# Eight columns fewer in the expert lists, and a looped general path, in a two-layer PEER decoder

## Chip, cores and metric

The kernel runs as one program on one core of one Trainium2 chip. Its time is the device time of one execution in microseconds (us). TensorE (PE) does matrix products from a stationary and a moving operand and adds them up in accumulators of 128 x 512 fp32; VectorE (DVE), ScalarE (ACT) and GpSimd (POOL) do the rest; DMA queues fed by SyncE (SP), ACT and POOL move data between DRAM and the core. Every engine runs its own list of instructions in order and waits on semaphores.

## The reference

Two post-norm layers on 256 tokens of width 1024, all in fp32. Layer 0 mixes tokens with a state-space block, layer 1 with attention; the change touches neither. Each mixer is followed by a PEER block: 16384 experts, each a row `u` and a row `v` of 1024 numbers. Every token picks 16 experts for each of 8 heads by product keys, and adds up their `v` rows, weighted with the gate and with gelu(x . u):

```python
best, pos = lax.top_k(cand, PEER_TOPK)
expert = jnp.take_along_axis(cidx, pos, axis=-1)
gate = jax.nn.softmax(best, axis=-1)
u_g = u[expert]
v_g = v[expert]
act = jax.nn.gelu(jnp.einsum('td,thkd->thk', xb, u_g).astype(f32))
return jnp.einsum('thk,thkd->td', (gate * act).astype(v_g.dtype), v_g)
```

A layer norm and a gated input (`x + sigmoid(x @ w_gate) * (p @ w_proj)`) end the layer.

## The kernel before

The program is mixer, `peer(0)`, mixer, `peer(1)`. In `peer` the 16384 experts are 128 columns of 128. A matrix of fp32 is always split into a high and a low half, `hi` by a cast on ScalarE and `lo` by a subtraction on VectorE (`split`, L124 and L125), and a product is three matmuls, high by high, high by low, low by high (`mm3`, L149).

**The u phase.** `expert_in(e)` (L908) runs for all 128 columns: it loads 512 KB of `u` over SP's queue, splits it, multiplies it with the tokens into one of four accumulators (`halves`, L161, 16 matmuls), and ScalarE copies the two halves of the accumulator out (L916, L917), POOL adds them with a DMA (L918), and gelu follows. Routing and gating run beside it. Matmuls at L979 mark which experts of the first `MANY` columns any token uses, with `MANY` as their width.

**The lists.** `listing` (L1018) puts the used experts of the first `MANY` columns into lists of three classes: used by both blocks of 128 tokens, by the first alone, by the second alone. A list is cut into groups of 128 experts; `CAPS` says how many groups a class has (38, 23 and 23), `BASES` where each class starts. The steps of `listing` are spread by hand over the last columns of `expert_in` and the first dense columns (`stages`, L1235).

**The v phase.** All output is accumulated in four accumulators, two blocks of tokens by two halves of the width. A column at or above `MANY` is dense: `dense(e)` (L1243) loads all its 128 rows of `v` (512 KB over SP's queue, `expert_load`), splits them and its weights, and multiplies, 12 matmuls of 128 x 512 (`expert_out`). A group is gathered: POOL issues two indirect DMAs, for the weight rows and for the 128 rows of `v` (`fetched`, L1175), both are split, and a group of class both takes 12 matmuls, one of the other classes 6 (`group_out`). There are four buffers for loaded rows, four for split ones and six for gathered rows.

**The order of the v phase** is a list of steps sorted by a fraction from 0 to 1 (`emit`, `spread_over`). The first `LEAD` (6) dense columns follow the u phase; then the groups of class one with `MIX` (13) dense columns among them; then the groups of class both and class two with the remaining dense columns, and among those, at set fractions, the loads of the layer norm's input and of seven matrices of the gate projection (`gate_load`), a branch hint at 0.04 and the branch at 0.1. The last five groups of class two come after that (`TAIL`), with the layer norm of the first block of tokens ahead of their matmuls.

**The branch** (L1210) reads a flag: if the lists were too short for the experts used, `general()` adds the surplus from all `MANY` columns. With this input the lists suffice, and the branch goes around it on every engine. Its body is a Python loop, so its 96 turns of 12 matmuls stand one after another in TensorE's list of instructions. `hint` marks for TensorE, ScalarE and VectorE where the branch will be and that it is likely taken.

```python
def branch(_):
    with self.after(self.pace.marks):
        surplus = nc.values_load(picked["flag"][:1, :1], min_val=0, max_val=1)
    with self.tc.If(surplus > 0, preferred_fallthrough_block=True, label=f"over{i}"):
        general()
    self.pace.marks = ()
```

Of the kernel before, what the change touches and what calls it, by code (L numbers as in the profile page):

```python
# [8 lines left out]
F32R = mybir.dt.float32r  # L9
F16 = mybir.dt.float16  # L10
U32 = mybir.dt.uint32
AF = mybir.ActivationFunctionType
# [5 lines left out]
P = 128  # L18
T = 256
# [6 lines left out]
TAIL = 5  # L26
TURNS = (3, 4, 1, 2)
SPLIT = ((0, 0), (0, 1), (1, 0))
MANY = 96
ROUTED = 56  # L30
GATED = 116
DIRECT = ROUTED - 8
LEAD = 6
MIX = 13
CAPS = (38, 23, 23)
BASES = (0, 38, 61)
GROUPS = sum(CAPS)
TOP = 32768.0

# [27 lines left out]
class Net:  # L67
# [73 lines left out]
    def plain(self, src):  # L141
        raw = self.raw()
        dma = self.nc.sync.dma_start(raw, src)
        self.pace.marks = (dma.ins,)
        return raw

    def mm3(self, out, lhs, rhs, start, stop):
        for i, (a, b) in enumerate(SPLIT):
# [236 lines left out]
    def tl(self, shape, tag, bufs, dt=F32):  # L385
        return self.pool.tile(shape, dt, tag=tag, bufs=bufs, name=self.name(tag))
# [364 lines left out]
    def peer(self, i):  # L751
        nc, dram = self.nc, self.dram
        with self.tc.tile_pool(name=f"peer{i}", bufs=1) as pool, ExitStack() as stack:
# [262 lines left out]
            picked = {}  # L1016
# [135 lines left out]
            def expert_load(e, w=None):  # L1152
                return weights(e) if w is None else w, self.chunk(dram["v"][i, e])

            def expert_out(w, hl, start):
                for tb in range(2):
                    for h in range(2):
                        self.mm3(accs[tb][h], lambda a: w[:, a, tb * P:(tb + 1) * P],
                                 lambda b: hl[:, b, h * 512:(h + 1) * 512], start, False)

            def fetched(s, hl=None):
                n = picked["n"] = picked["n"] + 1
# [24 lines left out]
                return kind, w, hl  # L1187

            def group_out(kind, w, hl, ends=()):
                for n, tb in enumerate(((0, 1), (0,), (1,))[kind]):  # L1190
                    for h in range(2):
                        self.mm3(accs[tb][h], lambda a: w[:, a, n * P:n * P + P],
                                 lambda b: hl[:, b, h * 512:(h + 1) * 512], False, tb in ends)

            def group(s):
                group_out(*group_load(s), (0,) if s == closing else ())

            def general():
                for c in range(MANY):
                    raw, part, some = x[:, c % 2], pp[:, c % 2, :T], pp[:, c % 2, T:2 * T]  # L1200
                    hl = wide[0][:, c % 2]
                    w = wide[0][:, 2 + c % 2, 0].rearrange("p (a t) -> p a t", a=4)[:, :2]
                    nc.scalar.dma_start(part, table[1 + c * P:1 + c * P + P, :])
                    nc.scalar.dma_start(raw, dram["v"][i, c])
                    nc.scalar.activation(some, part, AF.Identity, scale=picked["over"][:, c:c + 1])
# [11 lines left out]
            for hc in range(19):  # L1217
# [6 lines left out]
                if hc >= 7:  # L1224
# [10 lines left out]
            stages = [[classes], [*sums, ranks], [], [places, ones[0]], ones[1:3], ones[3:5], ones[5:7], ones[7:9], ones[9:11],  # L1235
                      [ones[11], surplus], [keys, one], [], [two], [both]]
# [6 lines left out]
            def dense(e):  # L1243
                if not begun:
                    begun.append(e)
                    accs.extend(self.accs())
                expert_out(*expert_load(e, ready.pop(e, None)), e == MANY)

            main = [lambda e=e: expert_in(e) for e in range(GATED, P)] + [lambda e=e: dense(e) for e in range(MANY, MANY + LEAD)]
            for n, step in enumerate(main):  # L1250
                step()
                if n == P - GATED - 1:
                    with self.after(self.pace.marks):
                        ready[MANY] = weights(MANY)
                with self.after(self.pace.marks):
                    for f in stages[n] if n < len(stages) else []:
                        f()
                    if n >= P - GATED + 3 and lates:
                        lates.pop(0)()
                    if n >= 2 and n % 3 and todo:  # L1260
                        todo.pop(0)()
# [32 lines left out]
            wide = [new([P, 4, 2, 1024], "wide", F32R)]  # L1294
            pgw = {}

            def gate_load(n):
                if len(wide) <= n // 4:
                    wide.append(tl([P, 4, 2, 1024], F32R, "high"))
                raw = (x, pp)[n // 2][:, n % 2] if n < 4 else None  # L1300
                pgw[divmod(n, 4)] = self.chunk(dram["w_pg"][i, n], hl=wide[n // 4][:, n % 4], raw=raw)

            loads = [(0.65, lambda: nc.sync.dma_start(x, self.x_d[i])), (0.7, lambda: nc.sync.dma_start(pp, self.pp_d[i])),
                     (0.75, lambda: self.load_gb(gb0, 2 * i + 1))]
            loads += [(at, lambda n=n: gate_load(n)) for n, at in enumerate((0.25, 0.35, 0.45, 0.55, 0.88, 0.92, 0.96))]
            emit(inner, spread_over(dense, range(MANY + LEAD + MIX, P), 0.86), [(at, extra, f) for at, f in loads],
                 [(0.04, hint, None), (0.1, branch, None)])
            end = []
            for k, s in enumerate(last):
                end.append(group_load(s, None if k else wide[1][:, 3]))  # L1310
# [141 lines left out]
```

## Time and profile before

| | us |
|---|---|
| median of 3 runs | 1874.46 (1873.03 to 1877.22) |
| profiled execution | 1863.86 |
| span of its profile | 1862.1 |
| TensorE busy in it | 1814.2 (97%) |
| VectorE, ScalarE, POOL busy | 1492.6, 1152.3, 629.7 |

The v phase of layer 0 runs from 667 to about 950 us of the span, that of layer 1 from 1553 to about 1836. In rows of groups and timelines, L149 with `acc<-hl,w` is a matmul of the v phase; `raw`, `hl` and `w` are the loaded rows, the split rows and the split weights. What stands in brackets is how long the engine was idle ahead of that row and what ended the wait: an engine with a name, a DMA, "issue" for idle time in which it waited for nothing that the profile shows, and PEq for TensorE's own sequencer. A window's "(x112)" counts the instructions in it, and PEclk is the share of full clock granted to TensorE.

### The profile page before, as it was taken

The page shows a single profiled execution, that of the slowest core. Times are in us where ns is not written, and L with a number is a line of the kernel's source. Part 1 is how long each engine was busy: PE and PEld are TensorE (multiplying, and loading weights), DVE is VectorE, ACT ScalarE, POOL GpSimd, SP SyncE. Part 2 cuts the span into 40 slices and gives each one's busy share as a digit, 9 for nine tenths or more (in the row PEclk, how much of TensorE's full clock was granted, in tenths as well). Part 3 has the DMA queues.
Part 4 walks back from the last instruction along what each step waited for, and adds up shares of the span by engine and source line. Part 5 has one row for each costly group of instructions (what it writes and reads, how often), then busy time and mean ns, then how long its engine had stood idle before and what let it go on. Part 6 is the DMA issues. An engine that isn't in the chain of part 4 may idle for free. (4 is left out here: it accounts for less than half of the span.)

```text
span 1862.1 us, 31749 instructions
## 1 busy us (share of the span) xinstructions
PE 1814.2 (97%) x11112; PEld 1542.1 (83%) x11112; DVE 1492.6 (80%) x2936; ACT 1152.3 (62%) x2330; POOL 629.7 (34%) x620
## 2 busy tenths in 40 slices
PE   8999999999999999799989999999999999989997
PEld 7998888888888877588878788888888887768876
DVE  7798789989989987466766878998998998747665
ACT  6865456696666656455646655669666666646553
POOL 0001013232222247767700001333222225767671
PEclk9999999999999999899999999999999999989999
DMA  7555669897699998888825556989779999889871
GB/s 271 201 184 186 215 184 228 216 249 192 185 281 332 287 303 282 274 299 301 271 104 193 198 189 185 228 217 248 198 184 278 332 283 316 284 269 316 293 228 61
DMA packets 217904, 444.29 MB, mean 239 GB/s; under 512 B 18980, under 2 KB 126664, under 8 KB 216072
## 3 DMA queue, kind: packets, MB, share of 16 engines
q1 hardware_dynamic: 75208, 266.75, 42.6%
q0 software_dynamic: 67648, 137.66, 28.7%
q10 hardware_dynamic: 74880, 37.75, 7.0%
q8 instruction: 91, 1.49, 0.3%
q14 instruction: 77, 0.63, 0.1%
HBM read 364.46 MB, written 44.08 MB: 219 GB/s over the span
## 5 line engine op out<-in xcount | busy, mean ns | idle before, releaser
L125 DVE TENSOR_TENSOR hl<-raw,hl 128x1024 fp32r<-128x1024 f32 x570 | 695.0, 1222 | 226.5 <-ACT hl L124 161.2
L161 PE MATMUL acc<-xT,hl 128*128 128x256 f32 (+1 forms) x4608 | 840.7, 340 | 1.4 <-DVE xT L188 0.8
L161 PEld LDWEIGHTS acc<-xT,hl 128*128 128x128 f32 x4608 | 700.6, 188 | 101.2 <-DVE hl L125 4.3
L124 ACT CAST hl<-raw 128x1024 fp32r<-128x1024 f32 x570 | 597.9, 1052 | 247.3 <-PE acc L149 105.9
L149 PE MATMUL acc<-hl,w 128*128 128x512 f32 x2220 | 524.9, 397 | 26.2 <-PEq L1213 9.3
L149 PEld LDWEIGHTS acc<-hl,w 128*128 128x128 f32 x2220 | 422.4, 191 | 127.2 <-issue 19.8
L918 POOL DMA_DIRECT2D w<-w x160 | 139.0, 869 | 399.4 <-ACT w L937 240.9
L918 POOL DMA_DIRECT2D act<-w x96 | 83.5, 870 | 302.8 <-ACT w L917 182.0
L1175 POOL DMA_INDIRECT raw<-in_v,r x136 | 156.9, 1154 | 73.4 <-issue 33.8
L916 ACT COPY w<-acc 128x256 f32<-128x256 f32 x160 | 59.7, 373 | 160.6 <-PE acc L161 156.7
L1175 POOL DMA_INDIRECT rows_w<-w_d,r x122 | 136.2, 1116 | 37.2 <-issue 36.3
L149 PE MATMUL mm<-xT,hl 128*128 128x256 f32 x816 | 100.8, 284 | 1.1 <-DVE hl L125 0.8
L149 PEld LDWEIGHTS mm<-xT,hl 128*128 128x128 f32 x816 | 98.5, 192 | 2.5 <-DVE hl L125 1.0
L917 ACT COPY w<-acc 128x256 f32<-128x256 f32 x256 | 97.5, 381 | 0.0
L962 DVE TENSOR_TENSOR pick<-pick,r 128x2048 f16<-128x2048 f16 x64 | 78.2, 1221 | 1.0
L916 ACT COPY act<-acc 128x256 f32<-128x256 f32 x96 | 35.6, 371 | 68.3 <-PE acc L161 67.9
L978 PEld LDWEIGHTS <-pick 128*128 128x128 f16 x1024 | 67.1, 98 | 13.0 <-issue 9.8
L979 PE MATMUL mm<-pick 128*128 128x96 f16 x512 | 67.5, 206 | 0.0
L214 POOL TENSOR_TENSOR ln_s<-ln_s,mhalf 128x1 f32<-128x1 f32 x8 | 4.4, 551 | 180.5 <-PE acc L149 131.0
L536 POOL TENSOR_TENSOR sq<-sq,sqt 128x256 f32<-128x256 f32 x12 | 12.5, 1039 | 149.1 <-ACT sqt L535 148.9
L978 PE MATMUL aux<-pick 128*128 128x128 f16 x688 | 59.3, 220 | 0.2
L1175 POOL DMA_INDIRECT pick<-a_d,r x46 | 52.4, 1139 | 19.6 <-issue 12.5
(290 smaller groups left out, 2109.8 us busy)
## 6 DMA issues: line engine op xcount, KB each, us to landing
raw<-in_u SPq DMA_DIRECT2D x256, 512.0 KB
raw<-in_v SPq DMA_DIRECT2D x64, 512.0 KB
w_d<-act ACTq DMA_DIRECT2D x48, 512.0 KB
w<-w POOLq DMA_DIRECT2D x160, 128.0 KB
raw<-in_w_q SPq DMA_DIRECT2D x32, 512.0 KB
raw<-in_w_xbc SPq DMA_DIRECT2D x24, 512.0 KB
act<-w POOLq DMA_DIRECT2D x96, 128.0 KB
a_d<-act ACTq DMA_DIRECT2D x24, 512.0 KB
```

The costliest lines, as they stand in the source:

```text
L124: a = self.nc.scalar.copy(hi, src)
L125: b = self.nc.vector.tensor_tensor(lo, src, hi.bitcast(F32), op=OP.subtract)
L149: self.last_mm = self.nc.tensor.matmul(out, lhs(a), rhs(b), start=start and i == 0, stop=stop and i == 2).ins
L161: self.nc.tensor.matmul(dst, hl[:, a, k * P:(k + 1) * P], src, start=k + a == 0, stop=(k, a) == order[-1] and k == KD - 1)
L536: nc.gpsimd.tensor_tensor(self.sq[g], self.sq[g], t, op=OP.add)
L916: nc.scalar.copy(whole, pe[:, :T])
L917: copied = nc.scalar.copy(pair[:, 1, :], pe[:, T:]).ins
L918: nc.gpsimd.dma_start(whole, pair[:, 1, :], accum_op=OP.add)
L962: nc.vector.tensor_tensor(a2, both, gates, op=OP.mult)
L978: nc.tensor.matmul(pg[:, t, :], one[:, 0, 4 * h + t], a2[:, 4 * h + t, k], start=k == 0, stop=k == 1)
L979: nc.tensor.matmul(banks["used"][:, MANY * tb:MANY * tb + MANY], one[:, 0, 4 * h + t], a2[:, 4 * h + t, 0, :MANY], start=at == 0, stop=at ...
L1175: got = nc.gpsimd.indirect_dma_start(out=dst, out_offset=None, in_=src, in_offset=rows(which))
```

## The change

1. `MANY` goes from 96 to 88 and `CAPS` from (38, 23, 23) to (36, 21, 21): 84 groups become 78, and 32 dense columns become 40, in each layer. The stages of `listing` are one step shorter.
2. The general path becomes a loop of the hardware (`For_i`) with one body of 12 matmuls, and the hint goes.
3. `mm3s` replaces `mm3` in the v phase: for all outputs of a column or group first high by high, then the weights' low half, then the rows' low half.
4. The first dense column's weights and rows are loaded and split inside `expert_in(127)`, ahead of the copies of that column (`expert_kept`); before, the weights alone were split, behind them.
5. The gate matrices 0 to 2 are loaded through other buffers, and the fourth comes at 0.87 instead of 0.55.

```diff
-MANY = 96
+LATE = ((0, 0), (1, 0), (0, 1))
+MANY = 88
-CAPS = (38, 23, 23)
-BASES = (0, 38, 61)
+CAPS = (36, 21, 21)
+BASES = (0, 36, 57)
...
+    def mm3s(self, outs, start, stop):
+        for i, (a, b) in enumerate(LATE):
+            for n, (out, lhs, rhs) in enumerate(outs):
+                self.last_mm = self.nc.tensor.matmul(out, lhs(a), rhs(b), start=start and i == 0, stop=stop(n) and i == 2).ins
...
                 self.halves(pe, self.chunk(dram["u"][i, e]), turned=e < 72)
+                if e == P - 1:
+                    with self.after(self.pace.marks):
+                        ready[MANY] = expert_load(MANY)
+                with self.after(self.pace.marks if e == P - 1 else ()):
+                    expert_kept(e, pe)
+
+            def expert_kept(e, pe):
                 pair = tl([P, 2, T], F32, "w", 5)
...
-                for c in range(MANY):
-                    raw, part, some = x[:, c % 2], pp[:, c % 2, :T], pp[:, c % 2, T:2 * T]
-                    hl = wide[0][:, c % 2]
-                    w = wide[0][:, 2 + c % 2, 0].rearrange("p (a t) -> p a t", a=4)[:, :2]
+                raw, part, some = x[:, 0], pp[:, 0, :T], pp[:, 0, T:2 * T]
+                hl, w = wide[0][:, 0], wide[0][:, 1, 0, :2 * T].rearrange("p (a t) -> p a t", a=2)
+                with self.tc.For_i(0, MANY, 1) as c:
...
-                      [ones[11], surplus], [keys, one], [], [two], [both]]
+            stages = [[classes], [*sums, ranks], [], [places, ones[0]], ones[1:3], ones[3:5], ones[5:7], ones[7:9], [*ones[9:11], surplus],
+                      [keys, one], [], [two], [both]]
...
-                if n == P - GATED - 1:
-                    with self.after(self.pace.marks):
-                        ready[MANY] = weights(MANY)
...
-            def hint(_):
-                with self.after(self.pace.marks[1:] + (self.last_mm,)):
-                    self.tc.mark_branch_hint_location(f"over{i}", "LikelyTaken",
-                                                      [e.engine for e in (nc.tensor, nc.scalar, nc.vector)])
...
-            loads += [(at, lambda n=n: gate_load(n)) for n, at in enumerate((0.25, 0.35, 0.45, 0.55, 0.88, 0.92, 0.96))]
+            loads += [(at, lambda n=n: gate_load(n)) for n, at in enumerate((0.25, 0.35, 0.45, 0.87, 0.9, 0.93, 0.96))]
             emit(inner, spread_over(dense, range(MANY + LEAD + MIX, P), 0.86), [(at, extra, f) for at, f in loads],
-                 [(0.04, hint, None), (0.1, branch, None)])
+                 [(0.1, branch, None)])
```

Around the branch of layer 0, TensorE's list before has the hint four steps ahead of the jump (three shown as one row are the three products of `mm3`; `wide` are the buffers of the general path):

```order
L1448 BRANCH_PREFETCH_HINT
L149 MATMUL acc_7960<-hl_8802,w_8803 128x512 x3
...
L149 MATMUL acc_7963<-hl_8858,w_8854 128x512 x3
L1212 TENSOR_LOAD r_902_7454
L1213 COMPARE_AND_BRANCH
L149 MATMUL acc_7960<-wide_8722 128x512
...
L1213 UNCONDITIONAL_BRANCH x2
```

The rows left out behind the jump are the 1152 matmuls of the body, each with its weight load. After the change the same place reads:

```order
L1223 TENSOR_LOAD r_902_7452
L1224 COMPARE_AND_BRANCH
L1213 COMPARE_AND_BRANCH
L1213 UNCONDITIONAL_BRANCH x2
L1452 BRANCH_PREFETCH_HINT
L151 MATMUL acc_7964<-wide_8682 128x512
...
L151 MATMUL acc_7967<-wide_8682 128x512
L1213 REGISTER_ALU
L1213 COMPARE_AND_BRANCH
L1213 UNCONDITIONAL_BRANCH
L1224 UNCONDITIONAL_BRANCH
```

The body is 12 matmuls now, and the hint that stands in it belongs to the loop, behind the jump.

At the first dense column of layer 0, ScalarE's list before has the copies of column 127 (`w_7950`) ahead of the cast of the dense column's weights (`w_7956`):

```order
L916 COPY w_7950<-acc_7928 128x256
L917 COPY w_7950<-acc_7928 128x256
L937 ACTIVATE w_7816<-w_7816 128x256
L124 CAST w_7956<-high_2361 128x256
L124 CAST hl_8051<-raw_8050 128x1024
```

After the change the first dense column's weights (`w_7939`) are cast ahead of the copies of column 127 (`w_7947`), with a cast of rows between them:

```order
L125 CAST w_7939<-high_2361 128x256
L125 CAST hl_8019<-raw_8018 128x1024
L929 COPY w_7947<-acc_7917 128x256
L930 COPY w_7947<-acc_7917 128x256
```

TensorE's list there, after the change, begins the column on three accumulators and comes to the fourth, `acc_7967`, as the sixth matmul:

```order
L167 MATMUL acc_7917<-xT,hl_7919 128x256
L151 MATMUL acc_7964<-hl_7943,w_7939 128x512
L151 MATMUL acc_7965<-hl_7943,w_7939 128x512
L151 MATMUL acc_7966<-hl_7943,w_7939 128x512
L151 MATMUL acc_7964<-hl_7943,w_7939 128x512
L151 MATMUL acc_7965<-hl_7943,w_7939 128x512
L151 MATMUL acc_7967<-hl_7943,w_7939 128x512
```

More of the change, by code (lines that the diff above doesn't have):

```diff
@@ L1150, in weights, with expert_load @@
                 return w
-            def expert_load(e, w=None):
-                return weights(e) if w is None else w, self.chunk(dram["v"][i, e])
+            def expert_load(e):
+                return weights(e), self.chunk(dram["v"][i, e])
             def expert_out(w, hl, start):
[L1156 to L1159, printed above, removed]
+                self.mm3s([(accs[tb][h], lambda a, tb=tb: w[:, a, tb * P:(tb + 1) * P],
+                            lambda b, h=h: hl[:, b, h * 512:(h + 1) * 512]) for tb in range(2) for h in range(2)],
+                          start, lambda n: False)
             def fetched(s, hl=None):
@@ L1189, in group_out @@
             def group_out(kind, w, hl, ends=()):
[L1190 to L1193, printed above, removed]
+                tbs = ((0, 1), (0,), (1,))[kind]
+                self.mm3s([(accs[tb][h], lambda a, n=n: w[:, a, n * P:n * P + P],
+                            lambda b, h=h: hl[:, b, h * 512:(h + 1) * 512]) for n, tb in enumerate(tbs) for h in range(2)],
+                          False, lambda n: tbs[n // 2] in ends)
             def group(s):
@@ L1198, in general @@
             def general():
-                for c in range(MANY):
-                    raw, part, some = x[:, c % 2], pp[:, c % 2, :T], pp[:, c % 2, T:2 * T]
-                    hl = wide[0][:, c % 2]
-                    w = wide[0][:, 2 + c % 2, 0].rearrange("p (a t) -> p a t", a=4)[:, :2]
-                    nc.scalar.dma_start(part, table[1 + c * P:1 + c * P + P, :])
-                    nc.scalar.dma_start(raw, dram["v"][i, c])
-                    nc.scalar.activation(some, part, AF.Identity, scale=picked["over"][:, c:c + 1])
+                raw, part, some = x[:, 0], pp[:, 0, :T], pp[:, 0, T:2 * T]
+                hl, w = wide[0][:, 0], wide[0][:, 1, 0, :2 * T].rearrange("p (a t) -> p a t", a=2)
+                with self.tc.For_i(0, MANY, 1) as c:
+                    nc.scalar.dma_start(part, table[bass.ds(1 + c * P, P), :])
+                    nc.scalar.dma_start(raw, dram["v"][i].rearrange("e p d -> (e p) d")[bass.ds(c * P, P), :])
+                    nc.scalar.activation(some, part, AF.Identity, scale=picked["over"][:, bass.ds(c, 1)])
                     self.split(w[:, 0], w[:, 1], some)
@@ L1234, in peer @@
             *ones, keys, both, one, two = steps[6:]
-            stages = [[classes], [*sums, ranks], [], [places, ones[0]], ones[1:3], ones[3:5], ones[5:7], ones[7:9], ones[9:11],
-                      [ones[11], surplus], [keys, one], [], [two], [both]]
+            stages = [[classes], [*sums, ranks], [], [places, ones[0]], ones[1:3], ones[3:5], ones[5:7], ones[7:9], [*ones[9:11], surplus],
+                      [keys, one], [], [two], [both]]
             assert kept[0] == MANY
@@ L1246, in dense @@
                     accs.extend(self.accs())
-                expert_out(*expert_load(e, ready.pop(e, None)), e == MANY)
+                expert_out(*(ready.pop(e, None) or expert_load(e)), e == MANY)
             main = [lambda e=e: expert_in(e) for e in range(GATED, P)] + [lambda e=e: dense(e) for e in range(MANY, MANY + LEAD)]
@@ L1293, in peer @@
             x, pp, gb0, gb1 = (new([P, 2, D], f"last{k}") for k in range(4))
-            wide = [new([P, 4, 2, 1024], "wide", F32R)]
+            wide = [new([P, 3, 2, 1024], "wide", F32R)]
             pgw = {}
             def gate_load(n):
[L1298 to L1301, printed above, removed]
+                if n == 3:
+                    wide.append(tl([P, 5, 2, 1024], F32R, "high"))
+                hl = wide[0][:, n] if n < 3 else wide[1][:, n - 3]
+                raw = (gb0, gb1)[n // 2][:, n % 2] if n < 3 else None
+                pgw[divmod(n, 4)] = self.chunk(dram["w_pg"][i, n], hl=hl, raw=raw)
             loads = [(0.65, lambda: nc.sync.dma_start(x, self.x_d[i])), (0.7, lambda: nc.sync.dma_start(pp, self.pp_d[i])),
                      (0.75, lambda: self.load_gb(gb0, 2 * i + 1))]
-            loads += [(at, lambda n=n: gate_load(n)) for n, at in enumerate((0.25, 0.35, 0.45, 0.55, 0.88, 0.92, 0.96))]
+            loads += [(at, lambda n=n: gate_load(n)) for n, at in enumerate((0.25, 0.35, 0.45, 0.87, 0.9, 0.93, 0.96))]
             emit(inner, spread_over(dense, range(MANY + LEAD + MIX, P), 0.86), [(at, extra, f) for at, f in loads],
-                 [(0.04, hint, None), (0.1, branch, None)])
+                 [(0.1, branch, None)])
             end = []
             for k, s in enumerate(last):
-                end.append(group_load(s, None if k else wide[1][:, 3]))
+                end.append(group_load(s, None if k else wide[1][:, 4]))
             dump = tl([P, D], F32, "pick", 2)
```

## Prediction

> **What bounds the kernel now.** I read the page first, its busy shares and its groups of instructions, then windows of 25 us over the stage that the change touches, then the timeline of TensorE wherever a window falls short. The profiled execution took 1863.86 us, 1.8 us more than its span of 1862.1; the median of the three runs is 1874.46, so 10.6 us above it. The sum below is made against 1863.86, and the 10.6 is put back at the end.
>
> ```profile
> PE 1814.2 (97%) x11112; PEld 1542.1 (83%) x11112; DVE 1492.6 (80%) x2936; ACT 1152.3 (62%) x2330; POOL 629.7 (34%) x620
> L125 DVE TENSOR_TENSOR hl<-raw,hl 128x1024 fp32r<-128x1024 f32 x570 | 695.0, 1222 | 226.5 <-ACT hl L124 161.2 <-issue 62.2 <-DVEq L1213 0.7
> L124 ACT CAST hl<-raw 128x1024 fp32r<-128x1024 f32 x570 | 597.9, 1052 | 247.3 <-PE acc L149 105.9
> L149 PE MATMUL acc<-hl,w 128*128 128x512 f32 x2220 | 524.9, 397 | 26.2 <-PEq L1213 9.3
> L1175 POOL DMA_INDIRECT raw<-in_v,r x136 | 156.9, 1154 | 73.4 <-issue 33.8
> L979 PE MATMUL mm<-pick 128*128 128x96 f16 x512 | 67.5, 206 | 0.0
> ```
>
> TensorE is busy for 97% of the span, so the end is set by how many matmuls there are and by the few places where TensorE stands. The L149 group is the v phase; its idle column names 9.3 us that TensorE's own sequencer takes at L1213, the branch around the general path. A window shows what such a place costs, because a full one holds 112 matmuls (columns: window, its length, then busy us and count of PE, PEld, DVE, ACT, POOL, then clock, DMA share, GB/s):
>
> ```profile
> 650.00:675.00 25.00, 22.90 (x160) 18.72 (x159) 20.91 (x61) 14.40 (x31) 9.82 (x11) 0.93 1.04 300
> 700.00:725.00 25.00, 24.79 (x109) 20.05 (x108) 17.49 (x26) 14.92 (x24) 19.00 (x16) 1.00 0.86 281
> 725.00:750.00 25.00, 24.42 (x106) 19.22 (x105) 17.13 (x25) 16.27 (x26) 19.76 (x16) 1.00 0.88 284
> 750.00:775.00 25.00, 22.43 (x91) 17.53 (x90) 14.83 (x21) 12.80 (x19) 19.52 (x19) 0.93 0.89 310
> 775.00:800.00 25.00, 15.83 (x62) 12.62 (x61) 10.34 (x14) 8.43 (x14) 15.04 (x14) 0.80 0.73 255
> 800.00:825.00 25.00, 25.00 (x112) 20.71 (x111) 17.81 (x23) 15.19 (x23) 18.07 (x18) 1.00 0.88 293
> 1600.00:1625.00 25.00, 24.04 (x103) 18.77 (x102) 17.27 (x25) 16.27 (x27) 18.51 (x17) 1.00 0.84 283
> 1625.00:1650.00 25.00, 24.14 (x105) 19.15 (x104) 16.03 (x22) 13.11 (x21) 19.42 (x18) 1.00 0.96 328
> 1650.00:1675.00 25.00, 19.30 (x55) 12.40 (x54) 10.45 (x14) 8.76 (x15) 15.60 (x16) 0.73 0.67 209
> 1700.00:1725.00 25.00, 25.00 (x112) 20.68 (x111) 15.75 (x22) 14.26 (x22) 18.56 (x16) 1.00 0.87 299
> 1775.00:1800.00 25.00, 23.16 (x101) 18.61 (x100) 17.66 (x22) 16.05 (x24) 16.76 (x15) 1.00 0.71 223
> 1800.00:1825.00 25.00, 24.86 (x110) 20.27 (x109) 16.04 (x25) 12.43 (x20) 16.60 (x15) 1.00 0.68 208
> ```
>
> The windows at 775 (50 matmuls short) and 1650 (57 short) hold the branch of layer 0 and of layer 1, and in both the granted clock is down as well. The windows around 700 to 775, 1600 to 1650 and 1775 to 1825 are short by 3, 6, 21, 9, 7, 11 and 2. At 800 and 1700 nothing is missing: with dense columns and groups mixed, VectorE and ScalarE have room there.
>
> **More matmuls.** A dense column and a group of class both are 12 matmuls of 128x512, a group of class one or two is 6. Per layer before: 32 x 12 + 38 x 12 + 46 x 6 = 1116; after: 40 x 12 + 36 x 12 + 42 x 6 = 1164. That is 48 more, 96 in all, and where TensorE is full each costs the pitch of its neighbours (timeline of TensorE, start, length, count):
>
> ```profile
> 917.80 17.16 PE L149 MATMUL acc<-hl,w 128*128 128x512 f32 x75
> ```
>
> The row ends one matmul after its last start, so the pitch is (17.16 - 0.397) / 74 = 0.2265 us; the full window says 25 / 112 = 0.223. I take the first: 96 x 0.2265 = **+21.7 us** (21.4 by the other). [...] New order inside a column (all high times high first) leaves count and weight loads as they are, at nothing.
>
> **Fewer used-marks.** The 512 matmuls of L979 go from 96 to 88 columns. At the pitch above 8 columns are 8/512 x 0.2265 = 3.5 ns, in all **-1.8 us** (nothing, if something other than columns paces them). Six groups fewer per layer free VectorE, ScalarE and POOL, which pays only where they are waited for, below. A dense column costs the same split of V as a group and a split of its weights like a group's, and its load goes to SP's queue where a group's goes to POOL's.
>
> **The branch.** Around it TensorE's timeline reads (idle time before and its releaser in brackets), first layer 0, then layer 1:
>
> ```profile
> 758.84 20.57 PE L149 MATMUL acc<-hl,w 128*128 128x512 f32 x83 [0.77 <-DVE hl L125]
> 788.58 17.64 PE L149 MATMUL acc<-hl,w 128*128 128x512 f32 x68 [9.17 <-PEq L1213]
> ```
>
> ```profile
> 1655.67 0.40 PE L149 MATMUL acc<-hl,w 128*128 128x512 f32 x1 [1.02 <-issue]
> 1657.78 2.90 PE L149 MATMUL acc<-hl,w 128*128 128x512 f32 x5 [1.72 <-issue]
> 1665.09 7.76 PE L149 MATMUL acc<-hl,w 128*128 128x512 f32 x23 [0.47 <-DVE hl L125]
> 1672.99 12.28 PE L149 MATMUL acc<-hl,w 128*128 128x512 f32 x53 [0.15 <-PEq L1213]
> ```
>
> In layer 0 TensorE stands 9.17 us at the jump over the unrolled path, and starts again at a lowered clock: 50 matmuls lost, 50 x 0.223 = 11.2 us. In layer 1 the jump itself is free (0.15), but between the hint and the jump matmuls come singly with nothing to wait for: 57 lost, 12.7 us, of which I give 0.4 to the two short waits for the split. I read both as one thing, TensorE's instructions arriving late: the body jumped over is 96 x 12 matmuls with a weight load each, 2304 instructions; the new one is 12 matmuls in a loop, 24 instructions and a few branches. With the hint and the long body gone I expect 0.3 us left per layer (the rows give 0.15 for a covered jump and 9.17 for the worst): 11.2 + 12.3 - 0.6 = **-22.9 us**. If the cover is not there, the whole term is lost. [...]
>
> **The first dense column.** Its weights and V row are now split ahead of expert 127's copies on ScalarE. TensorE waits there in each layer (layer 0, layer 1):
>
> ```profile
> 667.51 0.73 PE L149 MATMUL acc<-hl,w 128*128 128x512 f32 x2 [1.34 <-ACT w L124]
> 668.99 7.37 PE L149 MATMUL acc<-hl,w 128*128 128x512 f32 x24 [0.75 <-DVE w L125]
> ```
>
> ```profile
> 1553.43 0.73 PE L149 MATMUL acc<-hl,w 128*128 128x512 f32 x2 [1.34 <-ACT w L124]
> 1554.91 7.33 PE L149 MATMUL acc<-hl,w 128*128 128x512 f32 x31 [0.75 <-DVE w L125]
> ```
>
> That is 2.09 us per layer, and the window at 650 has clock 0.93, 25 x 0.07 = 1.75 us more in layer 0. What is queued behind the moved split: the copies of expert 127, delayed by one cast of V (1.05) and one of weights, which hold one of four accumulators. The first column meets that accumulator only as its sixth matmul, 1.1 us in. I leave 0.5 per layer for it and for the second column's weights, whose VectorE half stands behind the list stages: 4.2 + 1.75 - 1.0 = **-5.0 us** (0 to -5.9). SP's queue is in the same order as before, u of 127 and then the first v.
>
> **Gather-bound stretches.** The seven windows above without branch are short by 59 matmuls, 13.2 us. POOL is busy 19 to 19.8 of 25 us there; a group's two indirect gathers take it 1.154 us each and gaps, and six groups go per layer. A late V row also stops TensorE twice now, for its high half and 0.8 us later for its low half; with high times high first, the low half is needed only after 8 matmuls, 1.8 us on, instead of after one. These rows show both:
>
> ```profile
> 756.49 1.04 ACT L124 CAST hl<-raw 128x1024 fp32r<-128x1024 f32 x1 [2.09 <-DMA raw<-in_v,r]
> 757.58 0.49 PE L149 MATMUL acc<-hl,w 128*128 128x512 f32 x1 [1.78 <-ACT hl L124]
> ```
>
> The second stop (0.77) goes, the first (1.78) stays unless POOL's relief brings the gather sooner. I take half: **-6.6 us** (0 to -13.2).
>
> **The tail.** Before the turns into the gate projection TensorE waits for the layer norm, which stands on VectorE behind the split of the last tail group, whose gather lands late:
>
> ```profile
> 945.11 1.11 PE L185 MATMUL mm<-ident,last 128*128 128x128 f32 x4 [4.70 <-DVE last L220]
> 1825.42 1.05 ACT L124 CAST hl<-raw 128x1024 fp32r<-128x1024 f32 x1 [2.09 <-DMA raw<-in_v,r]
> 1830.98 1.12 PE L185 MATMUL mm<-ident,last 128*128 128x128 f32 x4 [5.11 <-DVE last L220]
> ```
>
> An earlier gather takes up to 2.1 us per layer off; the fourth late gate load adds a cast and a subtraction (1.05 + 1.22 = 2.3) to the same queues: I take -2.0 for the one and nothing for the other, since VectorE has 7 us of 25 free in these windows: **-2.0 us** (-4.2 to +4.6).
>
> **Sum.** 21.7 - 1.8 - 22.9 - 5.0 - 6.6 - 2.0 = -16.6. The profiled execution would be 1847.3, and the median 1874.46 - 16.6 = **1857.9 us**. The open ends of the three small terms (5.0, 6.6 and 6.6 up, 0.9, 6.6 and 2.2 down, taken as independent: 10.6 and 7.0) give 1850.9 to 1868.5 for this case.
>
> **Rivals.** (1) The jump costs the same with a short body: the sequencer stops at any taken branch on TensorE, and without the hint nothing fetches the landing. For it: the 9.17 in layer 0 came in spite of a hint. Against it: VectorE jumps over its own body at L1213 too, and its row above gives that 0.7 us for both layers. Then all 23.5 us of branch loss stay, only the added matmuls and the small gains count: -16.6 + 22.9 = +6.3, 1880.8 us, slower. It decides from a stop of about 9 us per layer on; at 6 the result is level. Chance 0.07. (2) Layer 1's single issues are not the hint's or the body's: there TensorE jumped free, and gathers and 0.67 of DMA share leave room for something else. Then 12.3 stay: 1870.2 us. For it: the two layers look unlike. Against it: the releaser is issue, not a wait, and it ends at the jump. Chance 0.13. (3) All standing goes: the mixed stretches run like the full windows at 800 and 1700, since 40 dense columns spread the gathers out, and the tail gains its 4.2. Then another 6.6 + 2.2 go: 1849.1 us. Chance 0.15. (4) The shorter lists overflow and the loop runs: each of its 88 turns is serial, at least 1.05 + 1.22 + 12 x 0.2265 = 5.0 us without its load, over 400 us per layer. Against it: counting this input's routing, layer 0 fills 34.8, 20.0 and 19.9 groups, layer 1 34.8, 20.0 and 20.1, of 36, 21 and 21. Chance 0.02.
>
> **Numbers.** The forecast has 0.63. A measurement here tells 0.2%, 3.7 us, from no change: faster below 1870.7, slower above 1878.2. Rival 3 is faster, rival 2 sits on the bound and is halved, rivals 1 and 4 are slower apart from 0.01. That gives faster 0.84, same 0.08, slower 0.08. The range from 1847 to 1871 takes in the forecast's ends, rival 3 and most of rival 2.
>
> **What would show it.** L151 should count about 96 matmuls more; the waits at L1224 and L1213 on TensorE should be under 1 us, and no single issues ahead of layer 1's branch; the first dense column should start with under 0.5 us idle. The forecast is wrong if a stop of several us stands at the jump, if windows beside it still hold under 100 matmuls, or if a new wait for the list stages, the last dense columns or the late gate loads takes the place of what went.

## The result, and the profile after

The changed kernel took 1861.11 us in the median of 14 runs (1849.60 to 1869.01), the kernel before 1872.98 us in 14 runs beside it (1863.70 to 1881.93): a ratio of 0.9937 with a 95% interval of 0.9913 to 0.9960, 11.9 us less. The forecast was 16.6 less. The profiled execution took 1855.82 us (span 1854.0), 8.0 below the profiled one of before. Both profiled executions lie below their medians, so the traces show a difference of 8 and the medians one of 12.

This first pair of sets was on one chip. The experiments ran on four chips (13, 9, 0 and 6), and there the kernel before took 1832.8 to 1834.4 us in the median of sets of 35, 21, 11 and 17 runs, 2% less, and never more than 1846.97. The record does not number the chip of the first sets; that it was a fifth is inferred from these levels. On one of the four the changed kernel was slower than the kernel before. Both results are told below, and they fit one account of the change, but for the cause of the first chip's stops, which stays open.

The windows of the changed kernel, cut as those of before (columns: window, length, busy us and count of PE, PEld, DVE, ACT, POOL, clock, DMA share, GB/s):

```profile
650.00:675.00 25.00, 24.52 (x169) 20.17 (x167) 22.72 (x66) 13.78 (x30) 10.85 (x12) 1.00 1.09 308
700.00:725.00 25.00, 24.86 (x109) 20.04 (x108) 15.78 (x23) 14.15 (x23) 17.86 (x15) 1.00 0.84 294
725.00:750.00 25.00, 24.52 (x107) 19.92 (x107) 18.18 (x27) 15.82 (x27) 19.45 (x17) 1.00 0.85 288
750.00:775.00 25.00, 24.01 (x106) 19.51 (x106) 18.39 (x25) 15.20 (x24) 19.82 (x18) 1.00 0.97 354
775.00:800.00 25.00, 24.10 (x107) 19.67 (x106) 14.23 (x20) 13.67 (x21) 15.98 (x16) 1.00 0.80 261
800.00:825.00 25.00, 25.00 (x112) 20.72 (x111) 17.90 (x24) 14.80 (x23) 16.14 (x16) 1.00 0.85 293
1550.00:1575.00 25.00, 22.71 (x94) 18.29 (x93) 16.48 (x30) 15.31 (x26) 11.06 (x11) 0.93 0.81 275
1600.00:1625.00 25.00, 23.81 (x103) 18.62 (x102) 15.47 (x23) 13.62 (x23) 18.81 (x16) 1.00 0.84 278
1625.00:1650.00 25.00, 22.50 (x97) 17.68 (x96) 14.60 (x20) 11.22 (x18) 19.52 (x19) 0.97 0.95 340
1650.00:1675.00 25.00, 23.77 (x88) 18.45 (x88) 15.11 (x21) 14.12 (x22) 15.70 (x14) 0.82 0.76 244
1775.00:1800.00 25.00, 25.00 (x112) 20.71 (x111) 20.17 (x27) 17.45 (x26) 16.73 (x15) 1.00 0.78 259
```

Layer 0 came out nearly as forecast: the window at 775 went from 62 matmuls to 107, and those from 700 to 775 lack 14 where they lacked 30. Layer 1 did not. The two windows from 1625 to 1675 lacked 64 and still lack 39, and at 1550, just behind the first dense column, the clock is down to 0.93. A full window still holds 112 (at 800): a matmul costs what it did.

TensorE's timeline of the changed kernel where the branch is, layer 0 and then layer 1 (start, length, count, idle time before and what ended it):

```profile
769.84 23.21 PE L151 MATMUL acc<-hl,w 128*128 128x512 f32 x100 [0.99 <-PE acc L151]
793.86 6.51 PE L151 MATMUL acc<-hl,w 128*128 128x512 f32 x28 [0.81 <-issue]
...
1623.33 22.44 PE L151 MATMUL acc<-hl,w 128*128 128x512 f32 x96 [1.07 <-ACT hl L125]
1647.37 0.96 PE L151 MATMUL acc<-hl,w 128*128 128x512 f32 x3 [1.60 <-issue]
1649.09 5.08 PE L151 MATMUL acc<-hl,w 128*128 128x512 f32 x9 [0.75 <-issue]
1655.26 25.12 PE L151 MATMUL acc<-hl,w 128*128 128x512 f32 x102 [1.09 <-PEq L1224]
```

The 9.17 us of layer 0 are gone; the jumps, at 769.84 and 1655.26, take 0.99 and 1.09 us. In layer 1 TensorE still stands ahead of the jump, by these rows for nothing (issue, 1.60 and 0.75), with no hint ahead of the jump and a short body, and the clock falls to 0.82. ScalarE, which splits the next rows, stands in the same places. First the kernel before, at its two branches:

```profile
788.34 1.05 ACT L124 CAST hl<-raw 128x1024 fp32r<-128x1024 f32 x1 [7.13 <-remote]
...
1662.73 1.04 ACT L124 CAST hl<-raw 128x1024 fp32r<-128x1024 f32 x1 [7.79 <-remote]
```

Then the changed kernel, in layer 1:

```profile
1646.28 1.04 ACT L125 CAST hl<-raw 128x1024 fp32r<-128x1024 f32 x1 [5.85 <-PE acc L151]
...
1654.13 1.04 ACT L125 CAST hl<-raw 128x1024 fp32r<-128x1024 f32 x1 [6.50 <-remote]
```

It idles 6 to 8 us each time, for three of them on something that the view cannot name (remote). The records of the trace behind the view name it: each of the four casts waits for one semaphore alone, which only TensorE's instructions raise (its matmuls, and one at the jump), and the wait for the landing of the rows had ended before (at 779.91 for the cast of 788.34). So ScalarE waited for TensorE here; the rows were not late. In layer 0 TensorE starts 0.24 us after that cast does, before the 1.05 us of the cast are over, so it did not need it. In the other three places TensorE goes on 1.09 to 1.13 us after ScalarE has begun, about as long as a cast takes: there the next rows were split only after TensorE had let ScalarE go. The 1.60 us at 1647.37 is such a turn, though its row says issue: the matmuls before end at 1645.77 (1623.33 + 22.44), and the cast runs from 1646.28 to 1647.32.

Nor do the trace's DMA packets show late instructions. The page of the kernel before has two queues of the kind instruction, q8 with 91 packets of 16 KB and q14 with 77 of 8 KB. q8 is taken for TensorE's here, by its beat of one packet every 26 to 34 us where TensorE runs full; that is a reading, which the page does not name. Around the stop of layer 0 its packets landed at 769.0 and 778.9, both before TensorE stopped at 779.41, and the next began at 789.9; around the single issues of layer 1 one landed at 1650.6 and the next began at 1670.7. What held TensorE from 779.41 to 788.58, and what spaced its single issues, stays open. (The record is not whole there: in the v phases of both traces of the first chip some updates of TensorE's semaphore are missing, 49 of 1029 before and 36 of 1049 after, and none in the traces of runs 1 to 8.)

The first dense columns after the change, TensorE in layer 0, TensorE in layer 1, then ScalarE in layer 1:

```profile
665.90 4.30 PE L151 MATMUL acc<-hl,w 128*128 128x512 f32 x16
670.54 4.83 PE L151 MATMUL acc<-hl,w 128*128 128x512 f32 x20 [0.33 <-DVE w L126]
675.89 24.33 PE L151 MATMUL acc<-hl,w 128*128 128x512 f32 x106 [0.53 <-ACT w L950]
```

```profile
1541.64 4.30 PE L151 MATMUL acc<-hl,w 128*128 128x512 f32 x16
1546.27 4.83 PE L151 MATMUL acc<-hl,w 128*128 128x512 f32 x20 [0.33 <-DVE w L126]
1553.39 26.95 PE L151 MATMUL acc<-hl,w 128*128 128x512 f32 x111 [2.29 <-ACT w L125]
```

```profile
1552.45 0.42 ACT L950 ACTIVATE w<-w 128x256 f32<-128x256 f32 x1 [5.22 <-DMA w<-w]
...
1552.93 0.71 ACT L125 CAST w<-high 128x256 fp32r<-128x256 f32 x2
```

The first column starts without a wait. Three columns on stands a new one: ScalarE waits 5.22 us for the accumulating DMA of the last u columns (its gelu, L950), and the cast of the next dense column's weights is queued behind that, so that TensorE waits 2.29 us, and after that its clock is down for a while (0.93 in the window). From the end of the u phase on, the first hundred matmuls of the v phase took 4.2 and 2.5 us more than a hundred times the pitch of 0.2265 before (layer 0, layer 1), and 1.8 and 5.1 after, so in the sum nothing was won. The new wait goes with the 88 columns, how is not shown: of the kernels below without copies, runs 4 and 6, with 88 columns, have it (0.46 to 1.27 us), and runs 3, 8 and 12, with the early first column and 96, do not. In run 12 the hundred are 0.7 and 0.6 us over their pitch:

```profile
666.23 3.91 PE L151 MATMUL acc<-hl,w 128*128 128x512 f32 x16
670.54 11.65 PE L151 MATMUL acc<-hl,w 128*128 128x512 f32 x50 [0.40 <-DVE w L126]
```

The turn into the gate projection, layer 0 and layer 1, waits less than half as long as before (4.70 and 5.11):

```profile
936.70 0.66 PE L191 MATMUL mm<-ident,last 128*128 128x128 f32 x4 [2.14 <-DVE last L226]
...
1822.35 0.74 PE L191 MATMUL mm<-ident,last 128*128 128x128 f32 x4 [1.90 <-DVE last L226]
```

That this is the work of the change is not shown: runs 1 and 2 below, which leave the tail as it was, have 2.00 and 1.84, and 1.92 and 1.60 there, and run 5, the kernel before, has 4.32 and 4.72.

The rows of the first dense matmuls and of the turns, before and after, cut the span into five stages, from first instruction to first dense matmul, to the layer norm's turn, to the first dense matmul of layer 1, to its turn, to the end:

| stage | before | after | difference |
|---|---|---|---|
| to the first dense matmul | 667.5 | 665.9 | -1.6 |
| v phase, layer 0 | 277.6 | 270.8 | -6.8 |
| from there to layer 1's | 608.3 | 604.9 | -3.4 |
| v phase, layer 1 | 277.6 | 280.7 | +3.1 |
| to the end | 31.1 | 31.7 | +0.6 |

Each v phase has 48 matmuls more, 10.9 us. Layer 0 won back 17.7 us of standing, layer 1 only 7.8.

### The profile page after: what moved, and what is told of

Its sections match the earlier page's. It is cut to its first block, busy times and chain, and to the rows that moved or that the text cites. A ratio compares the mean times of both kernels' runs of the same rounds, so it can differ in the third digit from the quotient of the medians.

```text
span 1854.0 us, 31864 instructions
## 1 busy us (share of the span) xinstructions
PE 1824.7 (98%) x11192; PEld 1554.5 (84%) x11192; DVE 1499.4 (81%) x2958; ACT 1157.6 (62%) x2322; POOL 604.0 (33%) x596
## 5 line engine op out<-in xcount | busy, mean ns | idle before, releaser
L126 DVE TENSOR_TENSOR hl<-raw,hl 128x1024 fp32r<-128x1024 f32 x578 | 706.8, 1225 | 207.4 <-ACT hl L125 148.7
L125 ACT CAST hl<-raw 128x1024 fp32r<-128x1024 f32 x578 | 606.3, 1052 | 226.6 <-PE acc L151 108.4
L151 PE MATMUL acc<-hl,w 128*128 128x512 f32 x2316 | 538.4, 393 | 11.2 <-issue 3.6
L151 PEld LDWEIGHTS acc<-hl,w 128*128 128x128 f32 x2316 | 437.1, 190 | 110.5 <-issue 7.7
L1187 POOL DMA_INDIRECT raw<-in_v,r x128 | 141.3, 1104 | 94.8 <-DVE hl L126 35.4
L1187 POOL DMA_INDIRECT rows_w<-w_d,r x114 | 132.1, 1159 | 34.7 <-issue 34.7
L991 PEld LDWEIGHTS <-pick 128*128 128x128 f16 x1024 | 66.4, 98 | 13.2 <-issue 11.1
L992 PE MATMUL mm<-pick 128*128 128x88 f16 x512 | 67.8, 203 | 0.0
L950 ACT ACTIVATE w<-w 128x256 f32<-128x256 f32 (+19 forms) x144 | 50.8, 353 | 8.7 <-DMA w<-w 8.7
```

What stands on the lines that cost most here:

```text
L125: a = self.nc.scalar.copy(hi, src)
L126: b = self.nc.vector.tensor_tensor(lo, src, hi.bitcast(F32), op=OP.subtract)
L151: self.last_mm = self.nc.tensor.matmul(out, lhs(a), rhs(b), start=start and i == 0, stop=stop(n) and i == 2).ins
L991: nc.tensor.matmul(pg[:, t, :], one[:, 0, 4 * h + t], a2[:, 4 * h + t, k], start=k == 0, stop=k == 1)
L992: nc.tensor.matmul(banks["used"][:, MANY * tb:MANY * tb + MANY], one[:, 0, 4 * h + t], a2[:, 4 * h + t, 0, :MANY], start=at == 0, stop=at ...
L1187: got = nc.gpsimd.indirect_dma_start(out=dst, out_offset=None, in_=src, in_offset=rows(which))
```

## The experiments

Every ratio is to the kernel before, run beside it on the same chip. Runs 1 to 4 shared one chip, 5 to 8 another, 9 and 10 a third, 11 and 12 a fourth.

**1. The loop alone, no hint, 96 columns.**

```diff
-                for c in range(MANY):
+                with self.tc.For_i(0, MANY, 1) as c:
...
-                 [(0.04, hint, None), (0.1, branch, None)])
+                 [(0.1, branch, None)])
```

> The kernel before with the looped general path and no hint, all else as before (96 columns listed). Theory A (TensorE's instructions came late because of the long body and the hint): both layers lose their stand at the branch, about 17 to 23 us, ratio to before 0.988 to 0.991, and neither PEq waits over 1.5 us nor single issues near the branch. Theory B (in layer 1 TensorE stood because gathered rows came late around the branch; only layer 0's jump was instructions): about 9 to 11 us, ratio 0.994 to 0.995, with half-clock matmuls near layer 1's branch.

Measured 1832.21 against 1834.36, ratio 0.9983 (0.9958 to 1.0007): not to be told from no change, a smaller gain than either theory's. The reason came with run 5: on these chips there was next to nothing to win at the jump.

**2. The hint alone taken away.**

```diff
-                 [(0.04, hint, None), (0.1, branch, None)])
+                 [(0.1, branch, None)])
```

> The kernel before without the hint, the general path still unrolled. If the hint caused the standing: 10 to 20 us gained, ratio 0.989 to 0.995. If the long body did, the landing must still be fetched in both layers: layer 0 keeps its 9 us and layer 1 trades its single issues for a jump of the same size, ratio 0.998 to 1.003. If the hint helped: slower by up to 10 us, ratio 1.005.

Measured 1842.29, ratio 1.0031 (1.0010 to 1.0052): 5.7 us slower. The hint had helped. The timeline of TensorE at the jump, layer 0, then layer 1:

```profile
780.41 19.97 PE L149 MATMUL acc<-hl,w 128*128 128x512 f32 x87 [1.35 <-PEq L1213]
...
1654.10 0.70 PE L149 MATMUL acc<-hl,w 128*128 128x512 f32 x2 [2.24 <-PEq L1213]
1658.34 6.94 PE L149 MATMUL acc<-hl,w 128*128 128x512 f32 x19 [3.53 <-issue]
```

Without a hint, a jump over the long body costs 1.35 us in one layer, and 2.24 and then 3.53 in the other. With the loop, in run 1, the same place has 0.15 us in both layers:

```profile
776.03 14.32 PE L149 MATMUL acc<-hl,w 128*128 128x512 f32 x62 [0.15 <-PEq L1212]
...
1649.44 5.93 PE L149 MATMUL acc<-hl,w 128*128 128x512 f32 x25 [0.15 <-PEq L1212]
```

In the packets, one of q8 goes with the hint. In the kernel before, TensorE's list comes to the hint at 765.67 and 1646.82, and a packet begins at 768.0 and 1649.6, 2.3 and 2.8 us later; in run 5 it is at 767.6, some 11 us ahead of the jump of layer 0, and here that one is missing. At the jump, the short body without the hint came out like the long one with it (0.15 us in runs 1 and 5); between runs 1 and 2 lies a ratio of 0.9983/1.0031 = 0.9952, 8.8 us on one chip.

**5. The kernel before once more,** for a trace.

> The kernel before, unchanged, for a trace on the same chip as the next three. If the standing at the branch belongs to the program, its trace shows about 9 us of PEq at L1213 in layer 0 and single issues in layer 1, as the first trace did; if it depends on how fast instructions and rows arrive on a chip, a chip on which the kernel takes about 1834 us shows under 4 us in the two layers together.

One run, 1843.90 us, beside a median of 1832.79 and a spread of 1826.58 to 1846.97 there. Its windows at the branch and TensorE's timeline there:

```profile
775.00:800.00 25.00, 24.85 (x111) 20.28 (x110) 16.46 (x23) 14.30 (x22) 19.51 (x19) 1.00 0.97 353
...
1650.00:1675.00 25.00, 24.83 (x109) 19.94 (x108) 15.80 (x22) 13.89 (x21) 19.99 (x17) 1.00 0.91 333
```

```profile
757.39 0.51 PE L149 MATMUL acc<-hl,w 128*128 128x512 f32 x1 [1.48 <-ACT hl L124]
758.65 20.69 PE L149 MATMUL acc<-hl,w 128*128 128x512 f32 x83 [0.76 <-DVE hl L125]
779.49 20.88 PE L149 MATMUL acc<-hl,w 128*128 128x512 f32 x91
```

Here 111 and 109 matmuls stand where the first trace had 62 and 55. The jump, at 779, takes 0.15 us, too little for the view to list, as does that of layer 1. The waits for late rows (1.48, then 0.76 for the low half) are there as before. Runs 7, 8 and 9, with an unrolled body (of 88 turns in run 7) and the same hint, show 0.15 us at each of their six jumps too. The loss at the branch, the largest term of the forecast, thus did not belong to the program alone: it came in the one trace from the first chip and in none of these four.

**6. The changed kernel once more.**

> The changed kernel, unchanged. Theory A (the gain belongs to the program): ratio to before 0.992 to 0.996 on this chip too. Theory C (the change trades 20 us of added matmuls for standing, and how much there is to trade depends on the chip): on a chip where before takes about 1834 us ratio 1.000 to 1.004, on one where it takes about 1873 us 0.991 to 0.996.

Measured 1841.87 against 1832.79, ratio 1.0054 (1.0038 to 1.0071): 9.9 us slower, outside both expectations, just above the second. Its group row of the v phase, beside that of run 5 (count, busy us, mean ns, and the idle time before them):

```profile
L149 PE MATMUL acc<-hl,w 128*128 128x512 f32 x2220 | 517.2, 394 | 13.9 <-DVE hl L125 5.5
```

```profile
L151 PE MATMUL acc<-hl,w 128*128 128x512 f32 x2316 | 529.8, 390 | 4.2 <-ACT w L125 2.3
```

It stands less, 4.2 us against 13.9, and against 11.2 for itself on the first chip. But busy time is up by 12.6 us. The two traces flatter the change: that of run 5 is of an execution 11.1 us above its median, that of run 6 of one 2.5 below, so the kernel before probably has less standing to win back, as a rule, than this one shows.

**7. The 88 columns alone,** with the stages and the gate loads that go with them; the lines that set the numbers:

```diff
-MANY = 96
+MANY = 88
-CAPS = (38, 23, 23)
+CAPS = (36, 21, 21)
-BASES = (0, 38, 61)
+BASES = (0, 36, 57)
```

> The kernel before with the 88 columns alone (with the changed gate loads), the general path unrolled with its hint and the order of products as before. By the pitch: 20 us slower, less what six groups fewer per layer give back. If they give back nothing: ratio 1.010 to 1.011. If they give back half of the 13 us of gather-bound standing: 1.006 to 1.008. If they give back all of it and the tail: 1.003.

Measured 1846.66, ratio 1.0072 (1.0049 to 1.0095): 13.2 us slower. 96 matmuls at 0.2265 us less the forecast's 1.8 for the marks were 19.9, so the columns gave back about 6.7 us by that, with an interval of 4.2 to either side: the case "half of the standing". That is net of a loss at the start: in its trace the first hundred matmuls of the v phase are 5.3 and 6.5 us over their pitch, against 4.1 and 2.5 in run 5.

**8. High by high first, and the early first column, with 96 columns.** The two parts were put in as the diff of the change has them.

> The kernel before with two parts alone, high by high first and the first dense column split early; 96 columns, unrolled path and hint stay. Forecast: 5.0 for the first column plus half of 13 us, 8 to 11 us less, ratio 0.994 to 0.996. If late rows stop TensorE whatever the order of the products, only the first column's 4 us: 0.998.

Measured 1829.36, ratio 0.9976 (0.9949 to 1.0002): 4.4 us less, the smaller of the two expectations, though the interval holds both. In its trace the first hundred matmuls of the v phase are 0.7 us over their pitch in each layer, where run 5 has 4.1 and 2.5. That is 5.3 us for the early first column, the forecast's 5.0, and leaves nothing of the 4.4 for the order of the products, within an interval of 5. The sum of runs 1, 7 and 8 (-3.1, +13.2, -4.4) is +5.7; the whole change measured +9.9.

**3 and 12. All but the 88 columns.** Loop, no hint, new order, early first column; 96 columns and the gate loads of before.

> All of the change but the 88 columns: loop, no hint, high by high first, early first dense column, with 96 columns listed and the gate loads of before. If the 96 added matmuls cost their pitch and nothing comes back, this is 20 us below the changed kernel: ratio to before 0.982 to 0.985. If fewer groups pay for the added matmuls (gathers come in time), it is level with the changed kernel: 0.992 to 0.995.

> All of the change but the 88 columns, without the copies, once more: ratio 0.995 to 0.9995, since the first time gave 0.9972. On a chip where the kernel before takes about 1873 us, 0.985 to 0.993.

Measured 0.9972 (0.9947 to 0.9998) and, on another chip, 0.9986 (0.9964 to 1.0009). Both figures of run 3's expectation, worked out from the first chip's 0.9937, were missed; that of run 12 held. With run 8 it is the fastest version of this study on these chips, 3 to 5 us below the kernel before, and set against run 6, on a third chip, by 1.0054/0.9979 = 1.0075 some 14 us below the changed kernel. The added matmuls were not paid for here.

**4. The changed kernel without the branch.** The general path is left out, so lists that are too short would lose experts.

```diff
-                 [(0.1, branch, None)])
```

> The changed kernel without the branch and the general path (the surplus of lists that are too short is left out). Theory A: the branch is nearly free now, within 3 us of the changed kernel, ratio to before 0.992 to 0.995. Theory B: the branch still drains the loads ahead of it (SyncE and POOL wait there for a split), and without it 7 to 10 us more go, ratio 0.988 to 0.990.

Measured 1837.16, ratio 1.0014 (0.9993 to 1.0035), above both figures. Set against run 6 (1.0054) it is 7 us less, as theory B had it, but that one is from another chip. The wait that theory B speaks of is in the trace of the changed kernel: at the branch of layer 1 SyncE issues nothing from 1637.82 to 1656.46 and waits 18.5 us of that for a split (DVE w L126). What that costs in the end is thus not settled. The trace is of use for another reason: TensorE hardly stands in it.

```profile
690.00:790.00 100.00, 100.00 (x442) 82.78 (x442) 72.28 (x98) 63.63 (x99) 76.13 (x69) 1.00 0.92 319
790.00:890.00 100.00, 100.00 (x443) 82.80 (x442) 65.57 (x86) 55.89 (x85) 62.55 (x55) 1.00 0.83 285
```

442 matmuls in 100 us are 0.226 us each, the forecast's 0.2265.

**9, 10 and 11. Copies among the loads.** Ahead of each dense column and each group ScalarE issues a copy of 64 KB from DRAM to DRAM; the copies are not part of the computation.

```diff
+            def more():
+                k, self.spared = self.spared, self.spared + 1
+                with self.after(self.pace.marks):
+                    nc.scalar.dma_start(self.spare[16 * k:16 * k + 16, :], dram["u"][i, k % P][:16, :])
...
             def weights(e):
+                more()
...
             def group_load(s, hl=None):
+                more()
                 kind, t, some, raw, hl = fetched(s, hl)
```

> The kernel before with a copy of 64 KB from DRAM to DRAM issued by ScalarE ahead of each dense column and each group, so that rows come later in the v phase (the copies are not part of the computation). Theory C (late rows and instructions make TensorE stand, and the changed kernel stands less): this kernel slows by 10 us or more and its PE idle in the v phases grows. If rows have slack everywhere: within 3 us of the kernel before, ratio 1.000 to 1.002.

> The changed kernel with the same copies. Theory C: it slows by less than half of what the kernel before slows by, so that the two come level or the changed one leads, where without the copies it was 9 us behind. If the added matmuls are all that counts: it stays 8 to 10 us behind the kernel before with the copies.

> All of the change but the 88 columns (the kernel of the third run), with the copies of 64 KB. If the 88 columns are what lets the changed kernel bear late rows, this one slows by as much as the kernel before did, 15 to 18 us, to a ratio of 1.006 or more. If the other parts (low half of the rows needed last, first column early) bear them, it slows by 9 us or less, ratio 1.000 to 1.003.

Measured: the kernel before with copies 1.0105 (1.0081 to 1.0128), the changed one 1.0097 (1.0073 to 1.0121), all but the 88 columns 1.0059 (1.0037 to 1.0081). Without copies they had 1, 1.0054 and, on the chip of the last, 0.9986. The copies so added 19.3, 7.9 and 13.4 us. Read like that, the changed kernel bears the copies best. They raised the DMA share of four windows of 100 us in the v phases from 0.72 to 0.91 (run 12) to 0.91 to 0.96 (run 11, on the same chip); how much later the rows came by that is not shown. But the copies did not stay in the v phase: in the kernels with 96 columns more of them were issued at the program's start (8 in the first 40 us of runs 9 and 11, 2 in run 10). First dense matmul of layer 0 in runs 9, 10, 11 and 12 (12 without copies):

```profile
673.26 0.96 PE L150 MATMUL acc<-hl,w 128*128 128x512 f32 x3 [1.35 <-ACT w L125]
```

```profile
664.44 4.20 PE L152 MATMUL acc<-hl,w 128*128 128x512 f32 x16
```

```profile
672.15 10.17 PE L152 MATMUL acc<-hl,w 128*128 128x512 f32 x42
```

```profile
666.23 3.91 PE L151 MATMUL acc<-hl,w 128*128 128x512 f32 x16
```

Run 11 comes 5.9 us later than run 12 there, run 9 some 5 us later than the kernel before (667.5 and 668.9 in its two traces), run 10 not at all. Less that, the copies cost 14, 8 and 7.5 us. With the copies the kernel before loses most, and the changed one comes level with it as measured (1850.92 and 1851.19 us); without the 5 us of early copies in the second it would stay some 5 us behind, by this estimate. That the 88 columns are not what bears the copies rests on the same correction: all but them then loses 7.5 us, within its expectation's 9, where the 13.4 as measured lies between its two cases. It stays in front either way.

## Why the prediction was right, and where not

Direction, range and the count of matmuls held on the chip on which the forecast was made; the gain was 11.9 us and not 16.6. That the time fell into the range is in part luck: the branch and the first column missed by 7 and 5 us, the tail helped without a cause that is shown, and on another chip the same change cost 9.9 us. Three of the signs that the prediction gave for being wrong came: single issues ahead of layer 1's branch, windows there with 97 and 88 matmuls, and a new wait behind the last columns of the u phase. By its steps, with the windows of the first chip:

- **More matmuls, 21.7.** Held. A full window has 112 before and after, and run 7 gives 13.2 us net for that part, gather relief included.
- **Used marks, -1.8.** Not seen. The mean length of one went from 206 to 203 ns, in both pairs of traces, but the 512 together were busy for 67.5 us before and 67.8 after; no run took them alone.
- **The branch, -22.9. This is the step that failed.** Its windows gave back 45 of 50 matmuls in layer 0 (10.0 us) and, with the window at 1625 into which the stand reaches, 25 of 64 in layer 1 (5.6), 15.6 in all. The prediction read the 9.17 us and the single issues of layer 1 as one thing, instructions that come late because of a long body and a hint, and as a property of the program. In layer 1 the standing stayed with neither of them, as the second rival had it. On two other chips the unrolled body with its hint takes 0.15 us at all eight jumps that were traced (runs 5, 7, 8 and 9). The hint, taken for a part of the trouble, is worth 5.7 us where the body is long (run 2); with the loop the jump takes 0.15 us, where the long body without a hint took 1.35 and 2.24. What stays open: what held TensorE on the first chip. The trace has neither late rows nor a packet of q8 on the way during these stops (from 778.9 to 789.9 and from 1650.6 to 1670.7 there is none), and no run of the study fell on that chip.
- **The first dense column, -5.0.** The wait for it went, and a new one came 10 to 12 us later (2.29 in layer 1, 0.53 in layer 0), behind a gelu that waits for a DMA (5.22 us in layer 1). Over the first hundred matmuls the two layers lost 6.7 us before and 6.9 after: net nothing. With 96 columns the part gives its 5 us (run 8). The prediction looked at who waits for column 127's copies on TensorE, and not at what is queued behind its gelu on ScalarE when the columns are 88.
- **Gather-bound stretches, -6.6.** Held in size: the windows from 700 to 775, at 1600 and at 1775 lacked 50 and lack 23, 6.0 us. Run 8 leaves next to nothing of it for the order of products. One reading was wrong: POOL's 19 to 19.8 us of 25 stand in four of the seven windows, and 18.5 at 1600 and 16.6 to 16.8 at 1775 and 1800.
- **The tail, -2.0.** The waits fell by 2.56 and 3.21 us, 5.8 in all, more than the bound of 4.2; runs 1 and 2 have waits as short without any change there.

Added up by the windows, 21.7 - 15.6 - 6.0 - 5.8 = -5.7, where the spans differ by 8.1 and the medians by 11.9; the rest is not accounted for. Rival 1 (the jump costs the same with a short body) is refuted: the jump over the loop shows 0.99 and 1.09 us on the first chip and 0.15 in run 1, where the rival needed about 9. A time above that of before came all the same on the second chip (1.0054), for a reason that no rival named: there was nothing to win at the branch, and 20 us of matmuls were added. That part of the account is shown by runs 5 to 9.

## What to carry to other kernels

A change that adds work to the engine that sets the end, to be paid for by waits that go, stands on the waits: take a second trace, on another chip if there is one, before counting them. Here the matmuls kept their pitch (0.2265 us on the first chip, 0.226 in run 4) and the wait did not come again (9.17 us at the jump of layer 0 in the first trace, 0.15 in run 5). The releaser that a row names is the wait that ended last; before its whole length is booked as a gain, look at the engine that makes the next operand, and where both stand at once, at which of the two waits for the other: here a wait that the view called remote was one for TensorE itself. Where a step is moved ahead on an in-order queue, look at the whole queue behind the step that it passes: here the gelu that waited 5.22 us for a DMA stood ahead of the cast for which TensorE waited 2.29. At the branch around the long unrolled body a hint and a loop did about the same on the numbered chips: 0.15 us at the jump with either (runs 5 and 1), 1.35 and 2.24 with neither (run 2).

## What the runs showed of the hardware

- One program took 1872.98 us in its first sets, on what seems a chip of its own, and 1832.8 to 1834.4 on four numbered ones, 2% apart, with scatters of 12 to 20 us in each set; verdicts on half a per cent did not carry from one to the other (0.9937 and 1.0054).
- A taken jump over 2304 instructions of TensorE cost 0.15 us in one layer and 9.17 in the other of one execution with a hint on the first chip, 0.15 at all eight jumps of four executions with a hint on two others (runs 5, 7 with 2112 instructions, 8 and 9), and 1.35 to 2.24 without a hint, with 3.53 more soon behind (run 2). Over a loop of 24 instructions, without a hint, it cost 0.15 (run 1), and 0.99 and 1.09 on the first chip.
- In the kernel before, a packet of 16 KB on the instruction queue q8 began 2.3 and 2.8 us after TensorE's hint (hint at 765.67 and 1646.82, packet at 768.0 and 1649.6). In run 5 the packet at 767.6 comes some 11 us ahead of the jump of layer 0 (at 779.4); in run 2, without the hint, that packet is missing.
